# The selected rows of the last four sequences: copied DRAM to DRAM by GpSimd's queue, read by SP as one transfer per unit

## The chip, the core and the metric

The kernel runs on one core of a Trainium2 chip. The core has five engines with an instruction queue each: TensorE (PE, with its weight loads shown apart as PEld), VectorE (DVE), ScalarE (ACT), GpSimd (POOL) and SyncE (SP, which here only issues transfers). Sixteen DMA engines move the data; SP, ACT and POOL hand them transfers on a queue of their own. The metric is the device time of one execution in microseconds, the median of several; less is better.

## The reference

One step of a one-layer decoder for a prompt of 512 tokens and a sample group of 8 sequences with 8 new tokens each, behind 2048 cached tokens. Both groups share the weights. Two attentions run side by side: a forgetting attention ("fox") over all cached keys and a sparse attention ("nsa") with compressed, selected and windowed keys. The cache lies in pages of 128 tokens, named by a page table.

```python
nsa_all = jnp.concatenate([gather_pages(nsa_pool, page_table), pm['nsa_rows']], axis=1)
kc, vc, c_end = compressed_kv(nsa_all[:, :, 0], nsa_all[:, :, 1], lp)
...
ks_blk = to_sel_blocks(nsa_all[:, :, 2], n_sel)
vs_blk = to_sel_blocks(nsa_all[:, :, 3], n_sel)
...
# cache_nsa_kv (DEPTH, N_PHYS, PAGE_SIZE, 4, NSA_GROUPS, HEAD_DIM): [cmp_k raw, cmp_v raw, slc_k, slc_v]
```

A cached row of `cache_nsa_kv` has 512 numbers of 4 bytes: columns 0 to 255 feed the compressed keys, columns 256 to 511 are the selected keys and values, the "selected rows" of the title. The kernel reads all of them for each sequence and masks the blocks that were not selected. A page thus has 128 pieces of 1 KB of selected rows, 128 KB in all; a sequence has 16 pages.

## The kernel before

The program is written with a layer that records all instructions, derives the waits, and puts each engine's instructions in an order by a simulated timeline. Some orders are pinned by hand: `dma` keeps the transfers that one queue issues in the order in which they are written (`issued`), and `link` chains PE's instructions in some stages.

The stages in order of time, by the profile: compressed keys of the cached pages (to about 164 us), projections of x (164 to 293), attention of the prompt (to about 440), attention of the sample (to about 560), merging (to about 715), output projection, MLP.

**Projections.** `run` calls `step(ci)` for ci = 0 to 7. A step multiplies all 576 rows of the normed x by some 260 columns of `w_in`. The product is made from a high and a low part of each operand: `project` splits the weights that were loaded during the step before (`winr`) into `winh` (on ACT) and `winl` (on DVE) in two halves of four slices each, asks for the next step's weights, and then runs 14 times 8 products for PE, tile after tile (`z`). ACT and DVE evict the tiles in turn, the sample's tile into `zS`, which lies in `r1w`. SP's queue carries in each step, in this order: `hfd` (a part of x is put aside, 576 KB), the weights of the next step (1 MB), `adw` (1 MB of `w_ada`), and from `stage()` eight copies of 128 KB: pages of `cache_fox_kv` are copied from DRAM to DRAM into `foxD`, in the layout in which the sample's attention reads them. `stage()` is called eight more times in the prompt's attention. The first instructions of the prompt's attention on POOL are the iotas `kpos` and `cm`, which DVE uses as soon as the projections are over.

**The sample's attention.** Its work is cut into 32 units: unit u is the sequence b = 2 (u // 8) + u % 2 and the quarter i = (u % 8) // 2 of its cached tokens, four pages. `sample_attention` takes two units at a time in 16 rounds s. `key_rows` turns the unit's fox and nsa keys on PE (`k<-identF,rows`), `pair_scores` makes the scores (`ss`), softmax runs on DVE and ACT (`sS`), `values` multiplies with the values, which lie in the same `rows` tile (`so<-rows,spT`). The tiles stand in 11 places that become free as PE finishes with them; `sample_load(u)` asks for unit u in round (u − 9) / 2. A load is one transfer of 512 KB from `foxD` (pieces of 4 KB), and four transfers of 128 KB from the pages of `cache_nsa_kv` (pieces of 1 KB), all on SP's queue. Before the four, SP reads the four page numbers from `ptp` into registers (`by_page`). At three of the 16 units from 16 on (u = 16, 26 and 28) the place is four smaller tiles, and the fox load is two transfers. SP waits before a transfer until the place is free, and until the transfer eight places earlier on its queue has landed.

In the last rounds `hH` (2.3 MB of x, put aside as `hfd`) and the merging's first weights (`graw`, `wbr`, `wmr`) are loaded too.

Of the kernel before, what the change touches and what calls it, by code (L numbers as in the profile page):

```python
# [6 lines left out]
F32 = mybir.dt.float32  # L7
# [7 lines left out]
P = 128  # L15
# [3 lines left out]
NB = 8  # L19
NS = 64  # L20
# [26 lines left out]
class Step:  # L47
# [626 lines left out]
    def stage(self):  # L674

        n = self.staged
        if n == 2 * NB:
            return
        self.staged += 1
        b, q = n // 2, n % 2  # L680
        self.by_page("sync", b, slice(8 * q, 8 * q + 8), lambda p, n: self.dma(
            "sync", self.foxD[b][8 * p:8 * p + 8].rearrange("q (y c) e -> (q y) (c e)", y=2),
            self.I["cache_fox_kv"][0, bass.ds(n, 1)].rearrange("o (q c) e g d -> (o q) (c e g d)", q=16)), 8)

    def stage_logf(self, pe, y):

        row = self.small.tile([P, 1], I32, tag="lfrow", bufs=2, name=f"lfrow{y}")
        self.ts(row, self.ptT, 2.0, float(y), OP.mult, OP.add)
        t = pe.tile([P, 512], F32, tag="lfg", bufs=1, name=f"lfg{y}")
        self.nc.gpsimd.indirect_dma_start(  # L690
            out=t, out_offset=None, in_=self.I["cache_fox_logf"][0].rearrange("n (y t) h -> (n y) (t h)", y=2),
            in_offset=bass.IndirectOffsetOnAxis(ap=row[:, 0:1], axis=0))
        self.lfg[y] = t
# [903 lines left out]
    def sample_load(self, sp, u):  # L1597

        p = u % 11
        where = {27: "6", 28: "5", 29: "8", 30: "9", 31: "a"}.get(u) or "pp23456879a"[p]  # L1600
        if u in (0, 11, 22):
            self.pair = self.keep.tile([P, 2, 2, 4, 256], F32, tag="r2", bufs=1, name=f"rows{u}")
        if where == "p":
            v = [self.pair[:, p]]
        elif where in "45":
            pool, tag = (self.pr, "kst") if where == "4" else (self.pkq, "qst")
            v = [pool.tile([P, 512], F32, tag=tag, bufs=4, name=f"rows{u}{x}").rearrange("p (j n) -> p j n", j=2) for x in range(4)]
        elif where == "3":
            v = [self.pr.tile([P, 2048], F32, tag="cm", bufs=1, name=f"rows{u}").rearrange("p (x j n) -> p x j n", x=2, j=4)]
        elif where == "7":  # L1610
            v = [self.zfp.tile([P, 4 * C_N], F32, tag="zF", bufs=1, name=f"rows{u}")[:, 0:2048].rearrange("p (x j n) -> p x j n", x=2, j=4)]
        else:
            pool = self.pr if where == "2" else self.sp0 if where == "6" else sp
            v = [pool.tile([P, 2, 4, 256], F32, tag="rows" + where, bufs=1, name=f"rows{u}")]
        b, i = 2 * (u // 8) + u % 2, u % 8 // 2
        row = (lambda n, j: v[0][:, n, j]) if len(v) == 1 else (lambda n, j: v[2 * n + j // 2][:, j % 2])
        for x in range(2) if len(v) > 1 else (None,):
            self.dma("sync", v[0][:, 0] if x is None else v[x],
                     self.foxD[b][:, 4 * i:4 * i + 4] if x is None else self.foxD[b][:, 4 * i + 2 * x:4 * i + 2 * x + 2])

        self.by_page("sync", b, slice(4 * i, 4 * i + 4), lambda p, n: self.dma(
            "sync", row(1, p % 4), self.I["cache_nsa_kv"][0, bass.ds(n, 1)].rearrange("o t e g d -> (o t) (e g d)")[:, 256:512]))
        self.rows[u] = row

    def window_load(self, sp, b):
# [878 lines left out]
    def run(self):  # L2504
# [11 lines left out]

        self.hfd = self.tc.dram_tile([P, NK, 2 * NT], F32, name="hfd")
        self.foxD = [self.tc.dram_tile([P, 16, 256], F32, name=f"foxD{b}") for b in range(NB)]
        self.lfD = self.tc.dram_tile([NB, P, P], F32, name="lfD")
        self.staged = 0  # L2520
        self.rows, self.wr, self.soft = {}, {}, {}
# [2 lines left out]
        h2 = []  # L2524
# [40 lines left out]
        with pctx:  # L2565
            pw, pc = self.pw, self.pc
            self.adn, self.ada_open, self.ada_next, self.ada_made = 8, None, None, None

            def step(ci, **kw):
                self.dma("sync", self.hfd[:, ci], h2[ci].bitcast(F32))  # L2570
                self.project(pw, ci, h2, **kw)
                self.ada_later()
                self.stage()

            step(0, between=[lambda: None] + [lambda kv=kv: self.cmp_out(None, 3, kv) for kv in range(2)] + [lambda: self.cmp_keys(3)])
            self.chain = None
            self.cmp_prompt_a(pk, pc)
            self.cmp_prompt_load(pk, 0)
            step(1)
            self.cmp_prompt_b(0)  # L2580
            self.cmp_prompt_load(pk, 1)
            self.head_norm("sk", C_SK, 2, 1)
            self.head_norm("wk", C_WK, 2, 2)
            step(2)
            self.cmp_prompt_b(1)
            self.head_norm("fk", C_FK, 2, 0)
            self.log_sigmoid()
            self.store_rows("fox", (C_FK, 256))
            step(3)
            self.cmp_prompt_c(pc)  # L2590
            self.head_norm("nq0", C_NQ, 4)
            self.gates()
            step(4)
            self.cmp_prompt_d(pc)
            self.head_norm("nq1", C_NQ + 256, 4)
            self.kslc = self.kstack(pk, "slc", C_SK, "w1")
            self.qnsa = {}
            step(5, between=[lambda: None] * 3 + [lambda: self.qnsa.update(self.qstack(self.pkq, "nsa", C_NQ, 1, 0, (0,)))])
            self.cmp_prompt_e(pc)
            self.head_norm("fq0", C_FQ, 4)  # L2600
            step(6, between=[lambda: self.qnsa.update(self.qstack(self.pkq, "nsa", C_NQ, 1, 0, (1,))), lambda: None,
                             lambda: self.sample_q(self.bdN, C_NQ, 1)])
            self.head_norm("fq1", C_FQ + 256, 4)
            step(7, between=[lambda: None] * 3 + [lambda: self.sample_q(self.bdF, C_FQ, 0)])
            self.store_rows("nsa", (C_CK, 256), (C_SK, 128), (C_SV, 128))
            self.store_rows("win", (C_WK, 128), (C_WV, 128))
            self.sample_kv()
# [89 lines left out]
```

## Time and profile before

| | |
|---|---|
| median of 3 runs | 1152.80 us (1152.79 to 1159.15) |
| profiled execution | 1153.68 us, of which 1152.0 us from the first to the last instruction |
| granted clock of TensorE | 0.999 |
| PE busy | 1130.2 us (98%) |
| DVE, ACT, POOL busy | 804.1, 580.5, 278.3 us |
| moved by the DMA engines | 255.5 MB, mean 222 GB/s |

A row of the profile's timeline has the start and the length in us, the engine, the line of the program, the operation, output<-input and shape, and in brackets the time for which the engine was idle before it and what ended that. Lines L78 and L84 are the helpers `mm` and `tr` (PE), L113 is `act`, L132 is `split`, L163 is `dma`: many groups share a line, so they are told apart by their tiles. SPq is SP's queue of instructions.

### The profile page before, as it was taken

What the parts mean: (1) busy time and instruction counts of PE and PEld (TensorE: products, weight loads), DVE (VectorE), ACT (ScalarE), POOL (GpSimd) and SP (SyncE); (2) the same over time, 40 slices, a digit from 0 to 9 for tenths busy, and PEclk for the clock granted to TensorE, in tenths of its full rate; (3) what the DMA queues carried; (4) which work ended last, traced back from release to release, by engine and by line L of the source; (5) the groups of instructions that cost most, each with busy time, mean ns of one, the idle gap of its engine ahead of it and who ended that gap; (6) DMA issues with size and microseconds to landing.
All of it is one profiled execution on the core that took longest, in us unless ns stands there. A gap on an engine that the chain in (4) does not pass through costs nothing.

```text
span 1152.0 us, 25217 instructions
## 1 busy us (share of the span) xinstructions
PE 1130.2 (98%) x9434; PEld 966.1 (84%) x9434; DVE 804.1 (70%) x1937; ACT 580.5 (50%) x1151; POOL 278.3 (24%) x337
## 2 busy tenths in 40 slices
PE   8999999999999999999999999999999999999998
PEld 5888789999756566776899999789999998888887
DVE  4688785687777895776755554677867754798686
ACT  2555463453776785565433223447565655565420
POOL 4302100000220120001576673010656411110100
PEclk9999999999999999999999999999999999999999
DMA  9997456797584779999889996446444637977732
GB/s 223 224 267 227 149 154 201 246 322 233 186 275 143 206 220 315 292 308 327 214 257 304 315 297 222 119 138 216 150 151 149 187 111 254 320 249 263 247 109 83
DMA packets 188188, 255.51 MB, mean 222 GB/s; under 512 B 23161, under 2 KB 144706, under 8 KB 185890
## 3 DMA queue, kind: packets, MB, share of 16 engines
q1 hardware_dynamic: 148770, 173.03, 49.4%
q0 software_dynamic: 21296, 67.38, 18.1%
q10 hardware_dynamic: 18000, 13.50, 3.9%
q8 instruction: 74, 1.21, 0.4%
q14 instruction: 48, 0.39, 0.1%
HBM read 217.64 MB, written 57.12 MB: 238 GB/s over the span
## 4 chain that ended last, share of the span: by engine, by line
PE 83%; DVE 7%; DMA 4%; issue 3%; ACT 2%; SPq 1%; POOL 1%; POOLq 0%; ACTq 0%; DVEq 0%
PE dn L78 14%; PE z L78 9%; PE mg L78 9%; PE hid L78 5%; PE br L78 4%; PE wo L78 4%; PE up L78 3%; PE k L84 2%; PE ct L84 2%; PE ada L78 2%; PE dns L78 2%; DMA rows<-in_cache_nsa_kv 2%; PE ss L78 1%; PE so L78 1%; PE oslc L78 1%
## 5 line engine op out<-in xcount | busy, mean ns | idle before, releaser
L78 PE MATMUL z<-winh,h 128*128 128x264 f32 (+1 forms) x576 | 110.9, 286 | 0.3
L78 PEld LDWEIGHTS z<-winh,h 128*128 128x128 f32 x576 | 91.7, 190 | 2.2 <-DVE h L808 0.9
L78 PE MATMUL z<-winl,h 128*128 128x264 f32 (+1 forms) x320 | 88.1, 284 | 0.0
L113 ACT ACTIVATE xh<-ct 128x256 fp32r<-128x256 f32 x128 | 48.0, 385 | 57.0 <-PE ct L84 32.2
L78 PE MATMUL mg<-hH,wmh 128*128 128x288 f32 x240 | 70.7, 296 | 0.0
L78 PE MATMUL mg<-hH,wml 128*128 128x288 f32 x240 | 70.5, 296 | 0.0
L78 PE MATMUL mg<-hL,wmh 128*128 128x288 f32 x240 | 68.4, 295 | 0.0
L132 DVE TENSOR_TENSOR xl<-ct,xh 128x256 fp32r<-128x256 f32 x128 | 51.8, 421 | 13.2 <-ACT xh L113 11.4
L78 PEld LDWEIGHTS z<-winl,h 128*128 128x128 f32 x320 | 60.6, 190 | 0.0
L132 DVE TENSOR_TENSOR wml<-wmr,wmh 128x1024 fp32r<-128x1024 f32 x14 | 23.4, 1675 | 37.2 <-ACT wmh L113 37.2
L78 PEld LDWEIGHTS mg<-hH,wmh 128*128 128x128 f32 x240 | 45.2, 188 | 0.1
L78 PEld LDWEIGHTS mg<-hH,wml 128*128 128x128 f32 x240 | 45.1, 188 | 0.0
L132 DVE TENSOR_TENSOR wp<-sums,wp 128x1024 fp32r<-128x1024 f32 x26 | 39.0, 1508 | 8.8 <-ACT wp L113 8.2
L78 PEld LDWEIGHTS mg<-hL,wmh 128*128 128x128 f32 x240 | 44.2, 188 | 0.0
L78 PE MATMUL hid<-xh,w1hlv 128*128 128x512 f32 (+1 forms) x160 | 43.6, 359 | 0.4 <-ACT xh L113 0.4
L78 PE MATMUL hid<-xh,w1hlk 128*128 128x512 f32 (+1 forms) x160 | 43.9, 361 | 0.1
L132 DVE TENSOR_TENSOR wp<-pu,wp 128x512 fp32r<-128x512 f32 (+1 forms) x26 | 29.4, 1138 | 17.0 <-ACT wp L113 16.9
L84 PE MATMUL k<-identF,rows 128*128 128x128 f32 x256 | 35.8, 280 | 3.2 <-ACT kt L113 1.5
L2062 POOL TENSOR_TENSOR td<-td,td 128x512 f32<-128x512 f32 x24 | 34.6, 1440 | 13.9 <-DMA td<-in_w_down 13.4
L78 PE MATMUL br<-oL,wbh 128*128 128x288 f32 x128 | 37.7, 295 | 0.0
L78 PE MATMUL br<-oH,wbl 128*128 128x288 f32 x128 | 37.7, 294 | 0.0
L84 PE MATMUL ct<-identF,ro 128*128 128x128 f32 x256 | 35.1, 275 | 2.6 <-DVE ro L116 2.4
(1178 smaller groups left out, 3618.0 us busy)
## 6 DMA issues: line engine op xcount, KB each, us to landing
adw<-in_w_ada SPq DMA_DIRECT2D x16, 1024.0 KB
foxD<-in_cache_fox_kv SPq DMA_DIRECT2D x128, 128.0 KB
rows<-in_cache_nsa_kv SPq DMA_DIRECT2D x128, 128.0 KB
rows<-foxD SPq DMA_DIRECT2D x26, 512.0 KB
pu<-in_w_up SPq DMA_DIRECT2D x26, 512.0 KB
wdr<-in_w_down SPq DMA_DIRECT2D x26, 512.0 KB
cpg<-in_cache_nsa_kv SPq DMA_DIRECT2D x96, 128.0 KB
td<-in_w_down POOLq DMA_DIRECT2D x24, 512.0 KB, 6.6
```

The source lines that it names most:

```text
L78: ins = self.nc.tensor.matmul(out, a, b, start=start, stop=stop, skip_group_check=True)
L84: ins = self.nc.tensor.transpose(out, in_, self.identF[:n, :n])
L113: return self.nc.scalar.activation(out, in_, f, **kw)
L132: self.splits.append((eng or self.nc.vector).tensor_tensor(l, x, h.bitcast(F32), op=OP.subtract).ins)
L2062: self.nc.gpsimd.tensor_tensor(out, x, y, op=OP.subtract)
```

## The change

For sequences 4 to 7 the selected rows are staged, as the fox rows are. At the start of each projection step a new function, `stage_rows(ci, made)`, copies eight pages of one sequence from DRAM to DRAM into `slcD`, on POOL's queue. A small copy (`late`) on POOL, of a number which the step before wrote into `zS`, holds each batch back until that step has left its columns; the first waits for the last part of x. In the sample's attention the units 16 to 31 read their 512 KB of selected rows from `slcD` in one transfer (two of 256 KB at units 16, 26 and 28), in pieces of 4 KB (2 KB). Units 0 to 15 are as before.

```diff
+    def stage_rows(self, ci, made):
+        late = self.small.tile([P, 1], F32, tag="late", bufs=1, name=f"late{ci}")
+        b, q = 4 + ci // 2, ci % 2
+        self.issued["gpsimd"] = self.nc.gpsimd.tensor_copy(late[:NS], made).ins
+        self.by_page("gpsimd", b, slice(8 * q, 8 * q + 8), lambda p, n: self.dma(
+            "gpsimd", self.slcD[b][p // 4, :, p % 4],
+            self.I["cache_nsa_kv"][0, bass.ds(n, 1)].rearrange("o t e g d -> (o t) (e g d)")[:, 256:512]), 8)
...
-        self.by_page("sync", b, slice(4 * i, 4 * i + 4), lambda p, n: self.dma(
-            "sync", row(1, p % 4), self.I["cache_nsa_kv"][0, bass.ds(n, 1)].rearrange("o t e g d -> (o t) (e g d)")[:, 256:512]))
+        if b in self.slcD:
+            for x in range(2) if len(v) > 1 else (None,):
+                self.dma("sync", v[0][:, 1] if x is None else v[2 + x],
+                         self.slcD[b][i] if x is None else self.slcD[b][i, :, 2 * x:2 * x + 2])
+        else:
+            self.by_page("sync", b, slice(4 * i, 4 * i + 4), lambda p, n: self.dma(
+                "sync", row(1, p % 4), self.I["cache_nsa_kv"][0, bass.ds(n, 1)].rearrange("o t e g d -> (o t) (e g d)")[:, 256:512]))
...
+        self.slcD = {b: self.tc.dram_tile([4, P, 4, 256], F32, name=f"slcD{b}") for b in range(4, NB)}
...
             def step(ci, **kw):
                 self.dma("sync", self.hfd[:, ci], h2[ci].bitcast(F32))
+                self.stage_rows(ci, self.zS[:, self.WIN[ci - 1][0]:][:, 0:1] if ci else h2[7][:NS, 0:1].bitcast(F32))
                 self.project(pw, ci, h2, **kw)
```

How instructions move, first on SP, in the sample's attention at unit 17 (the name behind "waits" is what the row waits for; DMAHW are transfers of SP's and ACT's queues, DMASW those of POOL's). Before:

```order
L163 DMA rows_7527<-foxD_84 128x1024 [waits DMAHW3_49,PE_49]
L170 TENSOR_LOAD ptp
L163 ISA
L163 DMA rows_7527<-in_cache_nsa_kv 128x256 [waits DMAHW4_49]
L163 ISA
L163 DMA rows_7527<-in_cache_nsa_kv 128x256 [waits DMAHW5_49]
L163 ISA
L163 DMA rows_7527<-in_cache_nsa_kv 128x256 [waits DMAHW6_49]
L163 ISA
L163 DMA rows_7527<-in_cache_nsa_kv 128x256 [waits DMAHW7_49]
L163 DMA rows_7542<-foxD_83 128x1024 [waits DMAHW0_49,PE_49]
```

And now, from the same unit on:

```order
L163 DMA rows_7736<-foxD_84 128x1024 [waits DMAHW1_49,PE_49]
L163 DMA rows_7736<-slcD_88 128x1024 [waits DMASW3_49,DMASW2_49,DMAHW2_49,DMASW1_49,DMASW0_49]
L163 DMA rows_7739<-foxD_83 128x1024 [waits DMAHW3_49,PE_49]
L163 DMA rows_7739<-slcD_87 128x1024 [waits DMASW7_49,DMASW6_49,DMAHW4_49,DMASW5_49,DMASW4_49]
L163 DMA rows_7875<-foxD_84 128x1024 [waits DMAHW5_49,PE_49]
```

Ten instructions of a unit have become two, and a unit takes two of SP's eight transfers in flight instead of five. A read of `slcD` also waits for the four copies that filled it.

On POOL, at the end of the projections, where the last batch stands. Before, `kpos` and `cm` followed the first iotas:

```order
L126 IOTA Dt 128x132
L126 IOTA kpos 128x512 [waits DMAHW5_49,DMAHW4_49,DMAHW6_49,DMAHW3_49,DMAHW7_49,DMAHW2_49,DMAHW0_49]
L126 IOTA cm 128x128 [waits DMASW6_49,DMASW7_49,DVE_49,PE_49]
L126 IOTA cm 128x128
L1065 TENSOR_SCALAR cm<-cm 128x128 [waits Pool_49]
```

Now the eight batches stand between `Dt` and `kpos`; these are the last two copies and what follows:

```order
L163 ISA
L163 DMA slcD_90<-in_cache_nsa_kv 128x256 [waits DMASW6_49]
L163 ISA
L163 DMA slcD_90<-in_cache_nsa_kv 128x256 [waits DMASW7_49]
L126 IOTA kpos 128x512 [waits DMAHW5_49,DMAHW4_49,DMAHW6_49,DMAHW3_49,DMAHW7_49,DMAHW2_49,DMAHW0_49]
L126 IOTA cm 128x128 [waits PE_49,Activation_49]
L126 IOTA cm 128x128
L1074 TENSOR_SCALAR cm<-cm 128x128 [waits Pool_49]
```

So 8 small copies, 8 reads of page numbers and 64 transfers went in ahead of `kpos` and `cm`, and each copy waits until the one eight places earlier has landed.

On ACT, in step 4 of the projections, where the weights of step 5 (`winr` 0 and 1) are split. Before:

```order
L113 ACTIVATE zN<-z_0_3462 128x256
L113 ACTIVATE r1w<-zN 128x256
L113 ACTIVATE winh_3707<-winr_0_3458 128x1024
L113 ACTIVATE r1w<-zN 128x256
L113 ACTIVATE winh_3707<-winr_1_3460 128x1024
L113 ACTIVATE zN<-z_2_3514 128x256
```

And now:

```order
L113 ACTIVATE zN<-z_0_3601 128x256
L113 ACTIVATE r1w<-zN 128x256 x2
L113 ACTIVATE zN<-z_2_3653 128x256
L113 ACTIVATE r1w<-zN 128x256
L113 ACTIVATE winh_3873<-winr_0_3597 128x1024
L113 ACTIVATE winh_3873<-winr_1_3599 128x1024
L113 ACTIVATE r1w<-zN 128x256
```

Both splits of the weights of step 5 now stand behind the eviction of z tile 2 (`zN<-z_2`) and a square of it. Steps 6 and 7 have similar moves; PE's own order is the same but for a few rows.

## The prediction

> **What bounds the kernel now.** I read the busy table first, then the stretches of the sample's attention, then the gaps of PE in it, then the chain of work behind them.
>
> ```profile
> span 1152.0 us, 25217 instructions
> PE 1130.2 (98%) x9434; PEld 966.1 (84%) x9434; DVE 804.1 (70%) x1937; ACT 580.5 (50%) x1151; POOL 278.3 (24%) x337
> ```
>
> PE is idle for 1152.0 − 1130.2 = 21.8 us in the whole span. No change of transfers can save more than the part of these 21.8 us that waits for transfers. So I ask how many of them lie in the stage whose loads change, and of what they are made.
>
> The view by stretches has length, busy us of PE, PEld, DVE, ACT and POOL, the granted clock, the DMA share and GB/s. The changed loads serve the units 16 to 31, which PE works through from about 500 us to 560 us:
>
> ```profile
> 480.00:520.00 40.00, 39.44 (x874) 29.61 (x864) 26.67 (x89) 23.89 (x54) 1.05 (x2) 1.00 0.93 305
> 520.00:540.00 20.00, 18.87 (x432) 14.02 (x433) 14.67 (x48) 10.73 (x26) 2.15 (x4) 1.00 0.93 309
> 540.00:561.00 21.00, 19.39 (x482) 14.02 (x472) 12.63 (x42) 10.68 (x22) 6.42 (x9) 1.00 0.83 236
> ```
>
> The DMA engines are 83 to 93% busy here, which looks like a memory bound; but PE is idle for only 0.56 + 1.13 + 1.61 = 3.30 us of 81. That is the ceiling of any gain in this stage. PE's timeline has these gaps over 0.25 us (in brackets the idle time and what ended it):
>
> ```profile
> 539.68 0.99 PE L78 MATMUL so<-rows,spT 128*32 128x64 f32 x56 [1.11 <-issue]
> 546.05 0.34 PE L78 MATMUL ss<-DT,E 96*32 96x128 bf16 x6 [0.29 <-issue]
> 551.08 0.33 PE L84 MATMUL k<-identF,rows 128*128 128x128 f32 x1 [0.59 <-DMA rows<-in_cache_nsa_kv]
> 556.54 0.66 PE L84 MATMUL sp<-identF,sS 128*128 128x128 f32 x4 [0.73 <-ACT sS L113]
> ```
>
> Only 0.59 us are a wait for selected rows. 1.11 + 0.29 = 1.40 us are gaps for which the profile names nothing; they fall in the stretch in which hH, the rows and the next weights are fetched together, so a busy DMA may be behind them. 0.73 us is the softmax of the last pair, with nothing left to cover it, and stays.
>
> How the 0.59 us arise, from SP's timeline (start, duration, four page transfers in a row) and the chain of work (start, us):
>
> ```profile
> 527.14 2.85 SPq L163 DMA_DIRECT2D rows<-in_cache_nsa_kv  x4
> 535.10 6.79 SPq L163 DMA_DIRECT2D rows<-in_cache_nsa_kv  x4
> 530.09 10.63 DMA rows<-foxD
> 541.55 9.49 DMA rows<-in_cache_nsa_kv
> ```
>
> SP needs 2.85 us for the four page issues of a unit, and 6.79 us for those of the last one, where it waits for earlier transfers to land. The last page of unit 31 is issued at 541.55 and lands 9.49 us later, just after PE asks for it.
>
> **The change part by part.** *Fewer issues on SP.* 16 units × 4 page transfers become 19 (13 units with one, three with two, since their buffer is in pieces). The issue of one costs little:
>
> ```profile
> L163 SPq DMA_DIRECT2D rows<-in_cache_nsa_kv x128: 332/333/1634, 414.0 to 541.5; - x128
> ```
>
> 45 × 0.33 = 15 us of SP's time go, and with them 16 reads of the page table. SP runs beside PE, so that is no time by itself; its worth is that a unit takes two places among SP's transfers in flight instead of five, and the last units are asked for earlier. The bytes are the same: 16 × 512 KB. Gain: at least 0 (the bytes still pass at the same rate), at most 3.30 − 0.73 = 2.57 us. I take the 0.59 us that the trace ties to these rows and half of the 1.40 us without a name, **−1.3 us**. If the cover goes the other way, and the loads now crowd hH, the cost is bounded by the same few tenths.
>
> *64 copies on POOL's queue during the projections.* Such a DRAM-to-DRAM copy from this queue is not in the trace; the nearest issue is that of the compressed pages at the start, of the same 128 KB, and the first eight of it:
>
> ```profile
> L163 POOL DMA_DIRECT2D cpg<-in_cache_nsa_kv x24: 529/529/809, 20.1 to 40.0; - x24
> 20.10 4.63 POOL L163 DMA_DIRECT2D cpg<-in_cache_nsa_kv  x8 [1.35 <-issue]
> 292.07 0.45 POOL L126 IOTA cm<- 128x128 f32 x2 [125.77 <-PE z L78]
> ```
>
> So a step's batch holds POOL for 0.2 (the copy `late`) + 1.35 (the page numbers) + 4.63 = 6.2 us, eight batches 50 us. POOL is idle for 125.77 us until 292.07, so they are covered there. Behind the last batch stand `kpos` and `cm`, for which DVE and PE wait after the projections. That batch starts when step 6 has left its columns:
>
> ```profile
> 278.00 0.37 ACT L113 ACTIVATE r1w<-z 64x256 f32<-64x256 f32 x1
> 245.78 0.41 DVE L101 TENSOR_TENSOR r1w<-z,r1w 64x256 f32<-64x256 f32 x1
> ```
>
> That is 278.00 + 0.37 + 0.41 = 278.8; 278.8 + 6.2 = 285.0, 7 us before 292.07: **0**.
>
> *The bytes of the copies.* A step copies 8 × 128 KB = 1.05 MB, on DMA engines that are nearly full in steps 4 and 5:
>
> ```profile
> 231.00:246.00 15.00, 15.00 (x138) 14.38 (x138) 11.45 (x37) 7.00 (x17) 0.00 (x0) 1.00 0.94 320
> 246.00:262.00 16.00, 16.00 (x144) 15.05 (x143) 14.50 (x53) 8.23 (x16) 0.00 (x0) 1.00 0.95 314
> 262.00:278.00 16.00, 16.00 (x140) 14.88 (x139) 11.91 (x35) 8.55 (x21) 0.00 (x0) 1.00 0.62 202
> ```
>
> At 314 / 0.95 = 330 GB/s, 1.05 MB take 3.2 us. This rate already holds copies of the same kind (foxD, one MB a step), so 3.2 us is the value that I take. Bounds: 0 where the copies fall into idle time, 6.4 us if read and write each count in full. Who waits for it? The weights of the next step: winr on SP's queue, split by ACT and DVE, then read by PE. Second halves, and the steps' starts on PE (chain of work):
>
> ```profile
> 241.84 1.06 ACT L113 ACTIVATE winh<-winr 128x1024 fp32r<-128x1024 f32 x1 [0.50 <-DMA winr<-in_w_in]
> 242.93 1.23 DVE L132 TENSOR_TENSOR winl<-winr,winh 128x1024 fp32r<-128x1024 f32 x1 [0.31 <-ACT winh L113]
> 254.73 1.23 DVE L132 TENSOR_TENSOR winl<-winr,winh 128x1024 fp32r<-128x1024 f32 x1 [0.15 <-ACT winh L113]
> 266.95 1.23 DVE L132 TENSOR_TENSOR winl<-winr,winh 128x1024 fp32r<-128x1024 f32 x1 [1.65 <-ACT winh L113]
> 246.29 11.51 PE z L78 x96
> 261.71 1.26 PE z L78 x9
> 277.90 11.70 PE z L78 x96
> ```
>
> 96 matmuls in 11.70 us are 0.122 us each. The second half of winh is first read by the 13th, of winl by the 15th: 1.7 us into the step. So the second half of winl is there at 244.16, 255.96 and 268.18, and is wanted at 248.0, 263.4 and 279.6: slack 3.8, 7.4 and 11.4 us for steps 5, 6 and 7. The batch of step 4 meets the weights of step 5, and what it delays stays delayed while the engines are full: delays of 3.2, 6.4 and 9.6 us. All three stay inside the slack, by 0.6, 1.0 and 1.8 us. Earlier batches meet emptier engines. With such thin margins I put **+0.5 us** for the projections, which is about what 4 us a batch would cost (0.2 at step 5, 0.4 at step 6).
>
> *The moved splits.* On ACT the two splits for step 5 now stand behind the eviction of z tile 2:
>
> ```profile
> 242.80 0.36 ACT L113 ACTIVATE zN<-z 128x256 f32<-128x256 f32 x1
> ```
>
> From 242.80: 0.4 for it, 0.4 for the square behind it, 2 × 1.06 and 1.23 give 246.9, still 1.1 us ahead of 248.0: **0**, and no addition to the delay, since ACT then waits for data that is late anyway.
>
> **Sum.** −1.3 + 0.5 = −0.8 us. The profiled execution took 1153.68 us (span 1152.0 and 1.7 around it), 0.88 above the median of 1152.80. So 1152.9 for an execution like it, and **1152.0** for the median.
>
> **Rivals.**
> *The projections become bound by transfers* (the slower side). Place: steps 5 to 7; it decides once a batch costs more than about 3.8 us of DMA time. At the upper bound of 6.4 us: 2.6 us of stall at step 5; at step 6 12.8 − 7.4 − 2.6 = 2.8; at step 7 19.2 − 11.4 − 5.4 = 2.4; together 7.8, so 1152.8 − 1.3 + 7.8 = 1159. For: 94 and 95% DMA share there. Against: foxD's copies already pass there, and PE has no gap.
> *The whole ceiling is won*: all gaps but the softmax tail go and nothing stalls: 1152.8 − 2.57 = 1150.
> *POOL's issues become slow beside DVE.* An issue would have to wait for DVE's copies. POOL has 292.07 − 278.8 − 1.55 = 11.7 us for the last batch, 1.46 us an issue; beyond that each further us an issue delays the start of the prompt's attention by up to 8 us. At 2.5 us: 1152.8 + 8 = 1161.
>
> ```profile
> L116 DVE COPY ro<-cpg x32: 629/689/987, 16.2 to 150.7; 128x1024 f32<-128x1024 f32 x32
> ```
>
> Against it: such copies of DVE ran in the very stretch in which POOL's 24 issues took 0.53 us, at most 0.81. The Trainium skill speaks for this rival: in "SBUF — State Buffer", section "SBUF: two separate sides", a DMA issued from GpSimd can't have its descriptors written while VectorE runs a two-port copy, and its example goes from 620 to 3100 ns; by that, an estimate from the page, eight issues would take 25 us and POOL would be 13 us late. The trace does not agree: 809 ns is the longest.
> *The copies are not used*, or SP waits for them: SP's reads of units 16 to 31 name the copies as their source, and the last copy, issued by 285, is long done at 480. Then the time would be that of before, 1152.8; it gives no other answer than the forecast.
>
> **How the numbers follow.** Forecast (within 2 us of 1152.0) 0.70; whole ceiling 0.10; projections bound 0.16; slow issues 0.02; neither, but the unchanged time 0.02. The range takes in the ceiling below and the upper price of the copies above: 1149.5 to 1159. About 1%, 11.5 us, is the least that a measurement of this kernel can tell from no change. Faster by that much would need over half of PE's 21.8 idle us: 0.01. Slower by over 1% needs prices beyond the upper bound or the slow issues: 0.05. The rest, 0.94, is no change.
>
> **What would show it.** After the change: PE's gap before `k<-identF,rows` near 551 gone; SP's reads of slcD 19 in number, with waits for PE (free buffers) in place of waits for transfers; 64 POOL issues of about 0.53 us ending before 286; DMA share near 1.0 from 231 to 270; ACT's wait for winr longer, but PE without a gap at the starts of steps 5 to 7. A PE wait for winl or winh there of more than 1 us makes the 3.2 us a batch wrong; a POOL row `cm` later than PE's end of z makes the cover wrong.

## The result and the profile after

The changed kernel takes 1166.1 us (median of 7, 1163.1 to 1170.1) against 1155.0 us (median of 7, 1152.8 to 1159.5): ratio 1.0101, 95% interval 1.0081 to 1.0121, slower by 11.7 us (9.4 to 14.0). The prediction had 1152.0 and a range up to 1159.0. The profiled execution took 1167.32 us, with a span of 1165.7. It is compared here with the profile of before, span 1152.0; the busy table first:

```profile
span 1165.7 us, 25259 instructions
PE 1136.9 (98%) x9434; PEld 970.9 (83%) x9434; DVE 797.6 (68%) x1937; ACT 580.2 (50%) x1151; POOL 322.6 (28%) x409
```

PE has the same 9434 matmuls, but is busy for 6.7 us more: a sign that some ran at a lower clock. Its idle time grew by 7.0 us, from 21.8 to 28.8. Where both lie is read from the starts of PE's stages (timeline of PE; first products of the projections, first scores of the prompt's attention, first turned keys of the sample's attention, first matmul of the merging). Before:

```profile
164.26 0.40 PE L78 MATMUL z<-winh,h 128*128 128x264 f32 x2
293.26 0.33 PE L78 MATMUL sslc<-khslc,qstnsa 128*128 128x128 f32 x1
440.52 0.66 PE L84 MATMUL k<-identF,rows 128*128 128x128 f32 x4
560.60 4.55 PE L78 MATMUL mg<-hH,w 128*128 128x288 f32 x32
```

And after:

```profile
164.65 0.40 PE L78 MATMUL z<-winh,h 128*128 128x264 f32 x2
301.26 0.33 PE L78 MATMUL sslc<-khslc,qstnsa 128*128 128x128 f32 x1
449.13 0.66 PE L84 MATMUL k<-identF,rows 128*128 128x128 f32 x4
572.51 4.55 PE L78 MATMUL mg<-hH,w 128*128 128x288 f32 x32
```

The projections take 136.6 us instead of 129.0 (+7.6), the prompt's attention 147.9 instead of 147.3 (+0.6), the sample's attention 123.4 instead of 120.1 (+3.3). The rest of the 13.7 us is 0.4 before the first product and 1.8 in small pieces behind 572 us.

**The projections.** The view by stretches (length, busy PE, PEld, DVE, ACT, POOL, granted clock, DMA share, GB/s), for the stretch in which step 4 begins:

```profile
231.00:246.00 15.00, 10.73 (x64) 10.40 (x64) 8.61 (x30) 6.01 (x15) 4.37 (x9) 0.77 0.98 328
```

PE is idle for 4.3 us of it and runs at a mean clock of 0.77; before, it was busy for all 15.00 at 1.00. Both count: 0.23 of 15 us, some 3.4 us of work, are lost to the clock, and with the idle time that makes the 7.6 us. The waits of PE (us in total, times, longest) name the gap:

```profile
PE z L78 <- ACT winh L113: 4.2, 1, 4.2
```

The chain of work (start, us) shows what it hangs on:

```profile
201.19 10.51 DMA winr<-in_w_in
...
214.44 1.26 DVE winl L132
...
222.81 0.82 DVE zF L101 x4
...
224.68 0.92 SPq L163
225.64 8.50 DMA winr<-in_w_in
234.16 1.06 ACT winh L113
235.27 1.22 PE z L78 x4
236.53 15.53 PE z L78 x108
...
254.29 11.51 PE z L78 x96
```

Read it downwards. The weights of step 3 land at 211.7, and the first split of them follows at 211.78, 4.0 us later than before. Their splits stand on DVE ahead of the normalised fox keys (`zF`), so these are ready at 223.6. SP issues in order: the store of `zF`, `hfd`, and only then the weights of step 4, at 225.64. They take 8.5 us, and PE starts step 4 at 235.27 instead of 230.63. In the kernel before, the rows of ACT (first split of step 3's weights), SP, ACT and DVE at the same place of the timeline read:

```profile
207.78 1.09 ACT L113 ACTIVATE winh<-winr 128x1056 fp32r<-128x1056 f32 x1 [2.48 <-DMA winr<-in_w_in]
...
222.42 1.80 SPq L163 DMA_DIRECT2D winr<-in_w_in  x2
...
228.40 1.06 ACT L113 ACTIVATE winh<-winr 128x1024 fp32r<-128x1024 f32 x1 [3.09 <-DMA winr<-in_w_in]
...
231.27 1.23 DVE L132 TENSOR_TENSOR winl<-winr,winh 128x1024 fp32r<-128x1024 f32 x1
```

So the request is 3.2 us later (0.4 of it because the projections start later), and the transfer takes 8.5 us instead of 6.0: together the first split of step 4's weights is 5.8 us late (234.16 against 228.40). The batches that do this are those of steps 2 and 3; POOL's timeline has the latter right beside the weights of step 4:

```profile
222.60 0.27 POOL L689 COPY late<-r1w 64x1 f32<-64x1 f32 x1 [19.26 <-DVE r1w L101]
223.82 4.52 POOL L163 DMA_DIRECT2D slcD<-in_cache_nsa_kv  x8 [0.95 <-issue]
...
291.97 4.53 POOL L163 DMA_DIRECT2D slcD<-in_cache_nsa_kv  x8 [0.18 <-issue]
...
300.13 0.45 POOL L126 IOTA cm<- 128x128 f32 x2 [3.05 <-PE z L78]
```

The last two rows answer for the cover: the last batch is issued by 296.5, and `cm` still waits for PE. From step 5 on PE has no gap; each step starts 8.0 us later than before (254.29 against 246.29).

**The sample's attention.** First by stretches:

```profile
480.00:520.00 40.00, 36.59 (x806) 26.75 (x805) 26.91 (x91) 21.12 (x49) 2.14 (x4) 0.98 0.88 315
520.00:540.00 20.00, 20.00 (x419) 14.84 (x418) 12.18 (x39) 10.70 (x22) 0.00 (x0) 0.96 0.80 281
```

And PE's gaps over 0.3 us with no name, from its timeline:

```profile
490.41 0.22 PE L78 MATMUL ss<-DT,E 96*32 96x128 bf16 x1 [1.46 <-issue]
...
508.87 0.66 PE L84 MATMUL k<-identF,rows 128*128 128x128 f32 x4 [0.42 <-issue]
...
516.62 0.53 PE L78 MATMUL so<-rows,spT 128*32 128x64 f32 x19 [1.53 <-issue]
...
546.99 0.41 PE L78 MATMUL so<-rows,spT 128*32 128x64 f32 x11 [0.34 <-issue]
```

The wait for selected rows near 551 us is gone. But the gaps for which the profile names nothing are now 1.46 + 0.42 + 1.53 + 0.34 = 3.75 us instead of 1.40, and the clock is at 0.98 and 0.96 instead of 1.00, which over 40 and 20 us is 1.6 us of work. In this profile 2.35 us more of such gaps and 1.6 us of clock, less the 0.59 us of the wait that went, are the 3.3 us. In the second profile of the kernel before (in the table below) the wait of 0.59 us is absent too, and the gap of 1.11 us is one of 0.20, so that they went is not by itself an effect of the change.

The 0.6 us of the prompt's attention stand in all ten profiles with batches of full size in steps 6 and 7 (147.8 to 147.9 us), and in none of the other six (147.2 to 147.4); their cause was not followed up.

### The profile page after: what moved, and what is told of

It reads as the page before. It is cut to its first block, busy times and chain, and to the rows that moved or that the text cites. A ratio compares the mean times of both kernels' runs of the same rounds, so it can differ in the third digit from the quotient of the medians.

```text
span 1165.7 us, 25259 instructions
## 1 busy us (share of the span) xinstructions
PE 1136.9 (98%) x9434; PEld 970.9 (83%) x9434; DVE 797.6 (68%) x1937; ACT 580.2 (50%) x1151; POOL 322.6 (28%) x409
## 4 chain that ended last, share of the span: by engine, by line
PE 82%; DVE 8%; DMA 5%; ACT 2%; issue 2%; SPq 0%; ACTq 0%; DVEq 0%
PE dn L78 12%; PE mg L78 9%; PE z L78 7%; PE hid L78 7%; PE br L78 4%; PE wo L78 4%; PE up L78 3%; PE k L84 3%; PE ct L84 2%; PE ss L78 2%; PE so L78 2%; DMA winr<-in_w_in 2%; PE ada L78 1%; PE sp L84 1%; PE oslc L78 1%
## 5 line engine op out<-in xcount | busy, mean ns | idle before, releaser
L78 PE MATMUL z<-winh,h 128*128 128x264 f32 (+1 forms) x576 | 113.6, 291 | 4.5 <-ACT winh L113 4.2
L132 DVE TENSOR_TENSOR wml<-wmr,wmh 128x1024 fp32r<-128x1024 f32 x14 | 19.0, 1356 | 41.4 <-ACT wmh L113 41.4
L2076 POOL TENSOR_TENSOR td<-td 128x512 f32<-128x512 f32 x24 | 36.9, 1542 | 15.9 <-DMA td<-in_w_down 15.7
L113 ACT ACTIVATE mgt<-mg 128x288 f32<-128x288 f32 x32 | 12.5, 407 | 52.9 <-PE mg L78 52.9
L113 ACT ACTIVATE u<-u 128x1152 f32<-128x1152 f32 x29 | 33.7, 1160 | 9.3 <-DVE u L101 8.7
```

Source lines behind the costliest of these rows:

```text
L78: ins = self.nc.tensor.matmul(out, a, b, start=start, stop=stop, skip_group_check=True)
L113: return self.nc.scalar.activation(out, in_, f, **kw)
L132: self.splits.append((eng or self.nc.vector).tensor_tensor(l, x, h.bitcast(F32), op=OP.subtract).ins)
L2076: self.nc.gpsimd.tensor_tensor(out, x, y, op=OP.subtract)
```

## Experiments

Theory A: there are two separate losses. The bytes of the copies make the weights of step 4 late, which costs the 7 to 8 us of the projections; the reads in the sample's attention cost something of their own. Rivals: the whole loss comes from the copies; it comes from the reads; not the bytes but the added issues and the shifted order do it. The table has the length of two stages (from the profile of each, as above) and the timed ratio to the kernel before.

| kernel | projections, us | sample's attention, us | ratio (95% interval) |
|---|---|---|---|
| before, two profiles | 129.0, 129.3 | 120.1, 118.9 | 1 |
| changed, two profiles | 136.6, 136.0 | 123.4, 122.1 | 1.0101 (1.0081 to 1.0121) and 1.0091 (1.0057 to 1.0124) |
| copies alone | 135.4 | 119.2 | 1.0071 (1.0044 to 1.0099) |
| reads alone | 129.8 | 118.1 | 1.0014 (0.9993 to 1.0035) |
| copies alone, a quarter of the bytes | 129.5 | 121.5 | 1.0028 (1.0006 to 1.0050) |
| copies alone, without steps 2 and 3 | 130.3 | 121.1 | 1.0028 (1.0003 to 1.0053) |
| copies alone, step 2 only | 132.5 | 119.5 | 1.0037 (1.0007 to 1.0066) |
| copies alone, step 3 only | 132.1 | 118.0 | 1.0022 (0.9999 to 1.0046) |
| whole change, batches behind the weights | 129.8 | 121.6 | 1.0043 (1.0028 to 1.0058) |
| whole change, batches moved | 129.1, 129.1 | 120.3, 121.3 | 1.0013 (0.9990 to 1.0037) and 1.0009 (0.9985 to 1.0034) |
| the same, pieces of 1 KB | 129.0 | 120.2 | 1.0019 (0.9997 to 1.0041) |
| batches moved, page reads | 129.3 | 120.6 | 1.0010 (0.9988 to 1.0031) |
| whole change, gap filled | 137.1 | 121.0 | 1.0090 (1.0054 to 1.0126) |

**Copies alone and reads alone.** The copies alone keep the page reads:

```diff
-        if b in self.slcD:
+        if False:
```

> The copies alone; the sample's attention reads the pages as before, and nothing reads the staged rows. Theory A (two separate losses: the copies make the weights of step 4 late, and the new reads of the sample's attention cost on their own): the projections end 8 us later, the sample's attention takes as long as before, so about +8 us on the kernel before (ratio near 1.007), with PE's 4 us gap before step 4 and a granted clock of 0.5 behind it. Theory B (everything comes from the copies, the loss in the sample's attention is only its echo): +12 us, ratio 1.010. Theory C (everything comes from the reads): no change.

The reads alone leave `stage_rows` out and read `foxD` twice:

```diff
-                self.stage_rows(ci, self.zS[:, ...)
...
-                         self.slcD[b][i] if x is None else self.slcD[b][i, :, 2 * x:2 * x + 2])
+                         self.foxD[b][:, 4 * i:4 * i + 4] if x is None else self.foxD[b][:, 4 * i + 2 * x:4 * i + 2 * x + 2])
```

> The reads alone: no copies, and units 16 to 31 read the same 512 KB of foxD a second time in place of their selected rows (so their selected keys and values are others). Theory A: the projections as before; the sample's attention 2 to 4 us longer, with PE gaps of over 1 us that the profile puts down to issue; ratio 1.002 to 1.003. My prediction's own step (fewer transfers on SP gain up to 1.3 us): ratio 0.999. Theory C: +12 us.

The copies alone cost 8.2 us by their ratio, with the same gap ahead of step 4 (PE's timeline), and leave the sample's attention as it was:

```profile
236.40 0.78 PE L78 MATMUL z<-winh,h 128*128 128x256 f32 x4 [3.96 <-ACT winh L113]
```

The reads alone cost nothing that can be told from no change (0.8 us less to 4 us more). In their profile the sample's attention took 118.1 us, 2.0 less than in the first profile of before and 0.8 less than in its second; the merging took 4.5 us more, with PE waiting for `oL` from DVE, which also happened in two other kernels (below). So the projections' part of theory A holds; a cost of the reads in this order of size does not show here.

**Bytes or issues.** A quarter of the rows of each page, with all 64 issues:

```diff
-            "gpsimd", self.slcD[b][p // 4, :, p % 4],
+            "gpsimd", self.slcD[b][p // 4, 0:32, p % 4],
...
-            ...rearrange("o t e g d -> (o t) (e g d)")[:, 256:512]), 8)
+            ...rearrange("o t e g d -> (o t) (e g d)")[0:32, 256:512]), 8)
```

> The copies alone, as in the run of the copies alone, with the same 64 issues on GpSimd's queue and the same waits, but only 32 of the 128 rows of a page are copied, so a quarter of the bytes (nothing reads them). Theory A (bytes): a batch takes 0.8 us of DMA time in place of 3.2, the weights of step 4 are at most 1.6 us late, PE's gap ahead of step 4 stays under 2 us and the clock stays at 1: ratio 1.000 to 1.002. Rival (the number of transfers on a second queue, or the order that the added instructions give the other engines): as the copies alone, ratio 1.007.

PE is busy through the whole stretch in which it waited, at full clock:

```profile
231.00:246.00 15.00, 15.00 (x132) 14.12 (x131) 10.43 (x32) 7.29 (x18) 4.16 (x9) 1.00 0.96 321
```

The projections take 129.5 us: it is the bytes (or the pieces of 1 KB, whose number fell with them), not the issues. The ratio is above what I expected. In its profile the merging took 162.6 us instead of 154, with PE waiting for `oL` from DVE; but that execution, of 1167.6 us, was the slowest of the ten, and where the median of 1159.9 us lost its 3 us (0.7 to 5.8) is not shown. The merging took 154.1 to 154.9 us in all other profiles but two (157.4, 158.6), also between two executions of the same kernel (154.2 and 157.4 with the batches moved), so the merging varies between single executions; the cause was not looked for.

**Which batches.** First without those of steps 2 and 3, then each of the two by itself (all with page reads):

```diff
-                self.stage_rows(ci, self.zS[:, ...)
+                if ci not in (2, 3):    # then: if ci == 2, if ci == 3
+                    self.stage_rows(ci, self.zS[:, ...)
```

> As the copies alone, but without the batches of steps 2 and 3 (sequence 5 isn't staged; the pages are read as before). Theory A, with the delay made by the batches of steps 2 and 3: step 4 starts as before, and the batches of steps 4 to 7 stay within the slack that I worked out for steps 5 to 7: no change, ratio within 0.001 of 1. Rival (each batch costs its share): 6 of 8 batches leave 6 of the 8 us, ratio 1.005.

> The copies alone, and of them only the batch of step 2 (nothing reads it). Theory A in its parts: this batch makes the weights of step 3 some 3 to 4 us late; their splits stand on DVE ahead of the norm of the fox keys, so out_fox and behind it the request for the weights of step 4 go out 3 us late on SP. Without the batch of step 3 nothing more is added: PE has a gap of 1 to 2.5 us ahead of step 4, under the length that lowers the clock; projections 130.5 to 132 us (before 129.0, with all copies 135.4 to 136.6), ratio 1.001 to 1.003. Rival (only the batch of step 3 counts, since it runs beside the weights of step 4): 129 us.

> The copies alone, and of them only the batch of step 3 (nothing reads it). Theory A: without the batch of step 2 everything of step 2 is in time, so this batch is released at about 219 us, in a stretch in which the DMA engines are nearly idle (share 0.01 to 0.29 at 214 to 222 us before), and is through before or soon after the weights of step 4 are asked for at 222.4: gap ahead of step 4 at most 1 us, projections 129 to 130 us, ratio 1.000 to 1.001. Rival (only the batch of step 3 counts): a gap of 3 us or more, projections 133 us or more.

Without the two, the projections lose 1.3 us instead of 6.4, and step 4 has no gap: six of the eight batches are nearly free there. The ratio of 1.0028 is above the expected 1.001, with an interval that reaches down to 1.0003; what it holds besides the 1.3 us is not shown. By itself, the batch of step 2 (SP's rows, then ACT's and PE's):

```profile
225.68 1.80 SPq L163 DMA_DIRECT2D winr<-in_w_in  x2
...
231.07 1.06 ACT L113 ACTIVATE winh<-winr 128x1024 fp32r<-128x1024 f32 x1 [4.03 <-DMA winr<-in_w_in]
...
232.18 0.78 PE L78 MATMUL z<-winh,h 128*128 128x256 f32 x4 [1.00 <-ACT winh L113]
233.44 0.39 PE L78 MATMUL z<-winl,h 128*128 128x256 f32 x1 [0.48 <-DVE winl L132]
```

And the batch of step 3:

```profile
222.97 1.11 SPq L163 DMA_DIRECT2D winr<-in_w_in  x2
...
232.10 1.06 ACT L113 ACTIVATE winh<-winr 128x1024 fp32r<-128x1024 f32 x1 [6.24 <-DMA winr<-in_w_in]
...
233.21 0.78 PE L78 MATMUL z<-winh,h 128*128 128x256 f32 x4 [2.03 <-ACT winh L113]
234.47 0.38 PE L78 MATMUL z<-winl,h 128*128 128x256 f32 x1 [0.48 <-DVE winl L132]
```

With step 2's batch the request goes out 3.3 us late (225.68) but the transfer is as quick as before (5.4 us); with step 3's the request is nearly in time (222.97) but the transfer takes 9.1 us. In both profiles the projections start 0.5 to 0.6 us later than in the first profile of before. The first batch delays through DVE and SP, the second through the DMA engines. The price of a batch is read from the transfers: step 3's batch makes the transfer of step 4's weights 3.1 us longer, and its own packets fill 29.5% of the 16 engines' time from 223 to 234 us, that is 3.2 us; step 2's batch makes the first split of step 3's weights 4.0 us later (211.8 against 207.8), or 3.4 without the later start.

What the projections lose, 3.5 and 3.1 us, comes near the same figure partly by chance. Step 2's 3.5 us are 1.5 of idle time and 2.0 in step 4's products, at a lower clock; step 3's 3.1 are 2.5 of idle time and 0.6 in the products. So the expectation for step 2's batch had the chain and the gap right, but not the clock, and its 130.5 to 132 us became 132.5. The expectation for step 3's batch failed: I had it released at 219 and through before or soon after the request; it was released at 219.9 and issued from 221.1 to 225.7, on both sides of the request at 222.97.

**Other places.** The whole change, first with `late` reading the next step's `winr`, then with four batches at the end of the compressed keys (issued from 137 to 163 us), two in steps 0 and 1 and two in steps 6 and 7:

```diff
-                self.stage_rows(ci, self.zS[:, ...)
                 self.project(pw, ci, h2, **kw)
+                self.stage_rows(ci, self.wraw[ci + 1][1][:NS, 0, 0:1] if ci < 7 else self.zS[:, ...)
```

> The whole change, but the small copy of step ci reads the second half of winr of step ci + 1, so a batch starts only when those weights have landed. Theory A: step 4 starts on PE within 0.5 us of before, the 8 us in the projections go, and the loss of the sample's attention stays: +2 to +4 us on the kernel before, ratio 1.002 to 1.004. Rival (the 8.4 MB as such cost the projections, wherever a batch falls: 8 x 3.2 us of DMA time on nearly full engines): adw and foxD push the next weights back instead, and step 5 or 6 has the gap; ratio 1.006 or more.

```diff
+        for k, u in enumerate((34, 35, 36, 38)):
+            todo[u] += [lambda k=k: self.stage_rows(k, self.ring[0][1][:NS, 0, 0:1].bitcast(F32))]
...
-                self.stage_rows(ci, self.zS[:, ...)
+                if ci in (0, 1, 6, 7):
+                    self.stage_rows(ci if ci > 5 else 4 + ci, self.zS[:, ...)
```

> The whole change, with the same eight batches at other places: four at the end of the compressed keys (from about 135 us, DMA share 0.5 and below in the trace of before), two in steps 0 and 1, two in steps 6 and 7; none in steps 2 to 5. Theory A: the projections take 129 us as before (136.6 in the changed kernel, 129.8 with the batches held behind the weights); what is left is the sample's attention, between the 2.0 us that the reads alone gained and the 3.3 us that the changed kernel lost there: ratio 0.998 to 1.002. Rival (a batch costs wherever it stands): ratio 1.004 or more, as with the batches held behind the weights.

Both free the projections (129.8 and 129.1 us). In the first all 8.4 MB still pass there, so the bytes as such cost at most 0.8 us. The moved batches are 0.8 to 0.9% faster than the changed kernel and not to be told from the kernel before; no version ran faster than that one. The first variant is still 5 us slower (3.2 to 6.7), of which 0.8 lie in the projections and 1.5 in the sample's attention of its profile; the rest is not pinned down.

**What is left: the reads.** A second profile of the changed kernel, the staged rows in pieces of 1 KB (`slcD` page by page, still one transfer a unit), and, with the moved batches, page reads against staged reads:

> The changed kernel once more, for a second profile: does the loss of the sample's attention (123.4 us against 120.1) come back with PE gaps of over 1 us that end on issue, each just behind a transfer of PE's instructions, or do these gaps fall elsewhere in each execution? If they belong to the reads in pieces of 4 KB: again 2 to 4 us of such gaps between 480 and 560 us. If they are chance: another sum, and the stage within 1 us of 120. Projections: again 136 to 137 us, ratio 1.010.

```diff
-        self.slcD = {b: self.tc.dram_tile([4, P, 4, 256], ...
+        self.slcD = {b: self.tc.dram_tile([4, 4, P, 256], ...
...
-            "gpsimd", self.slcD[b][p // 4, :, p % 4],
+            "gpsimd", self.slcD[b][p // 4, p % 4],
...
-                         self.slcD[b][i] if x is None else ...)
+                         (self.slcD[b][i] if x is None else ...).rearrange("j p e -> p j e"))
```

> As the moved batches, but the staged rows lie page by page, so that the reads of units 16 to 31 are still one transfer of 512 KB, in pieces of 1 KB as before the change. If the PE gaps on issue come from bursts of 4 KB pieces that fill the DMA engines (over 400 GB/s, share 1.0) while PE's instructions are fetched: no such gap over 0.5 us between 440 and 545 us, and the stage takes 119 to 120 us. If the number of transfers matters (fewer, larger ones): as the moved batches. Ratio 0.998 to 1.001.

> The moved batches (four at the end of the compressed keys, two in steps 0 and 1, two in steps 6 and 7), but the sample's attention reads the pages as before, and nothing reads the staged rows. This is the other half of the comparison with the moved batches: only the reads of units 16 to 31 differ. If the staged reads cost something of their own: this kernel is 1 to 3 us faster than the moved batches with staged reads, and its sample's attention takes 118 to 121 us. If the staged reads gain what I predicted: it is 1.3 us slower. Ratio on the kernel before 0.999 to 1.001.

> The moved batches with the staged reads once more, beside the same kernel with page reads. If the staged reads cost: the sample's attention again above 120 us (120.2 to 123.4 so far), ratio 1.001 to 1.003. If they gain 1.3 us: below the kernel with page reads, ratio under 1.

Timed, page and staged reads can't be told apart: 1.0010 and 1.0009, each uncertain by about 0.0023, which is more than the 1.3 us that I had predicted. By the profiles in the table, the stage took 120.2 to 123.4 us with reads of `slcD` (seven profiles, mean 121.4) and 118.0 to 121.5 us with page reads (eight, mean 119.9); the reads alone, which read `foxD` in the same pieces, took 118.1. A wait of PE for selected rows stands in three of the eight (0.6 to 2.3 us) and in none of the seven, so the staged reads do seem to remove it. A cost of 1 to 2 us in the stage may be there all the same; a gain does not show, and the timing alone could not exclude one of 1.3 us. The gaps on issue of the second profile of the changed kernel, then of the pieces of 1 KB:

```profile
508.86 0.66 PE L84 MATMUL k<-identF,rows 128*128 128x128 f32 x4 [2.07 <-issue]
...
515.52 0.53 PE L78 MATMUL so<-rows,spT 128*32 128x64 f32 x19 [0.43 <-issue]
...
545.29 0.41 PE L78 MATMUL so<-rows,spT 128*32 128x64 f32 x11 [0.89 <-issue]
```

```profile
538.20 0.41 PE L78 MATMUL so<-rows,spT 128*32 128x64 f32 x10 [1.32 <-issue]
```

They come at the same places of PE's program as in the first profile (`k` x4, `so` x19, `so` x11), inside runs of equal instructions, with other lengths each time. Pieces of 1 KB do not remove them (1.32 us), so that expectation failed too. In the traces of all 16 profiles, each of the 42 such gaps of 0.2 us or more in this stage ends 1.2 to 1.8 us behind the end of one of the 16 KB transfers of instructions, which pass through the same DMA engines, some 6 us apart. So these gaps are most likely waits of PE for its instructions, with the page reads too; but no run here changes those transfers, so this is not shown by experiment, and why the staged reads should lengthen the waits stays open.

**The clock behind the gap.** 20 matmuls into a bank that nothing reads, between the last work ahead of step 4 and its first product:

```diff
+        if ci == 4:
+            with self.tc.issue_after(self.last_z):
+                self.cmp_warm(20)
```

> The whole change, and 20 more matmuls of 128x512 bf16 into a bank that nothing reads, between the last PE work ahead of step 4 and its first product (4.3 us by the same matmuls at the start). They fill the gap in which PE waits for the weights. If the granted clock of 0.5 behind the gap is a result of the idle time: the clock stays at 1, the products of step 4 take 13.4 us again, and the projections take 133 us in place of 136.0 to 136.6: ratio 3 us lower, 1.007. If the clock is something else (the DMA load, chance), the projections stay at 136 us or more.

PE's rows:

```profile
230.21 4.48 PE L78 MATMUL idle<-identB 128*128 128x512 bf16 x20
235.19 0.51 PE L78 MATMUL z<-winh,h 128*128 128x256 f32 x2 [0.49 <-ACT zN L113]
...
253.32 0.50 PE L78 MATMUL z<-winh,h 128*128 128x256 f32 x2 [0.43 <-DVE zN L116]
```

And the stretch:

```profile
231.00:246.00 15.00, 13.94 (x99) 11.31 (x97) 8.97 (x30) 5.60 (x14) 4.39 (x9) 1.00 0.97 328
```

Without the idle time the clock stays at 1.00, so the drop follows from it. But the time did not come back: the projections took 137.1 us and not the expected 133. Ahead of the gap this profile is 0.7 us earlier than that of the changed kernel; at the end of step 4's products it is 2.1 us ahead, and at the start of step 5 again only 0.7, after new waits for evictions (0.43 us above, 0.50 just before), for which the bank that the filling takes may be to blame. What the low clock costs in the end is thus not settled; within the gap's step it is 3.4 us (from 235.27 to 252.06, 16.8 us for the products of step 4, against 13.4 before).

## Why the prediction was wrong

- **Fewer issues on SP, −1.3 us: not borne out.** SP's reads of `slcD` are 19, and the 0.59 us wait for rows near 551 went, as forecast; but it is not in the second profile of the kernel before either. The 1.40 us without a name, of which I took half as won, did not go: such gaps are 3.75 us in the profile, and by the instruction transfers behind which they end they were hardly waits for rows. The moved batches, which leave only the reads to count, are 0.1% slower than before, uncertain by 0.2%.
- **The batches on POOL, 0: right.** The issues took 0.52 to 0.60 us. They ended at 296.5 us and not before 286, since the steps came 8 us later; `cm` still waited for PE. This also settles the rival of slow issues beside DVE: nothing like 1.46 us occurred.

```profile
L163 POOL DMA_DIRECT2D slcD<-in_cache_nsa_kv x64: 523/523/596, 169.6 to 296.0; - x64
```

- **The bytes, +0.5 us: the price was right, the place was wrong.** 3.2 us a batch stands against 3.1 us (step 3's batch) and 3.4 us (step 2's) by which one batch by itself delayed a transfer of weights. For steps 5 to 7 the slack held: without the batches of steps 2 and 3, the four of steps 4 to 7 gave PE no wait for weights. The step that failed is the sentence "Earlier batches meet emptier engines", which put the earlier batches at nothing; the projections lost 7.6 us in place of 0.5. I worked out the slack of steps 5, 6 and 7 and not that of step 4. The row was there: the second half of `winl` ends at 231.27 + 1.23 = 232.5, and is wanted 1.7 us behind the step's start at 230.63, that is at 232.3. By that rule step 4 has no slack at all, and the engines are not emptier where it counts. In the kernel before, by stretches:

```profile
202.00:214.00 12.00, 12.00 (x113) 11.25 (x114) 8.88 (x36) 4.79 (x10) 0.00 (x0) 1.00 1.02 336
214.00:222.00 8.00, 8.00 (x81) 7.83 (x78) 5.80 (x33) 4.28 (x9) 0.00 (x0) 1.00 0.13 30
222.00:234.00 12.00, 12.00 (x108) 11.25 (x108) 6.03 (x19) 5.81 (x16) 0.00 (x0) 1.00 1.01 333
```

  A DMA share of 0.81 over 200 to 240 us looked like room, but it is full, empty, full, and both full stretches are those in which weights come. Two batches of 3.2 us come close to the 5.8 us by which the first split of step 4's weights was late.
- **The order of the queues was not followed.** I followed each batch to the next step's weights, and took a delay there to be a delay of PE only. The batch of step 2 found no waiting PE at step 3, but moved DVE's splits, DVE's work behind them, and through SP's in-order queue the request for the weights of step 4. It also moved its own successor: batch 3 is released by step 2's last columns (`late` at 222.60 instead of 219.9 with that batch alone).
- **The moved splits on ACT, 0: right.** No gap at the starts of steps 5 to 7.
- **The rivals.** "The projections become bound by transfers" named the right mechanism, and that its 7.8 us are near the 7.6 measured is luck: it stood at steps 5 to 7, with a deciding price of 3.8 us a batch, where none of it occurred. At step 4 any price decides. With 0.16 for it, and a range that ended at its 1159 with the reads' gain taken off, the outcome of 1166 had no place.
- **What would show it.** The line that a wait of over 1 us for `winh` makes the batch's price wrong misled in one point: the wait came, a step earlier, with the price right.
- **A lower clock behind a gap** was no term of the sum. Of the 7.6 us of the projections 4.2 are the gap ahead of step 4, and 3.4 are step 4's products at the lower clock.

## What to carry to other kernels

When a transfer is added to a stage with double-buffered weights, work out the slack of every step, from the rows of its last split and of its first use, and above all of the steps in which the DMA engines look idle: a mean share says nothing about the moment at which the next weights are asked for. Follow a late transfer through the in-order queues of the engines that consume it, since what stands behind it may be the request for the next one. Copies that only have to be done some time belong in a stretch that is empty and asks for nothing; here this alone took back all of the projections' 7 us, and a gain at the reading end still did not show.

## What the hardware showed beside this

PE's clock halved after idle time that was shorter than I had expected, and not after other idle time that was longer. The changed kernel behind its gap of 4.2 us (from 242 us on the clock was at 1.00 again):

```profile
236.00:238.00 2.00, 1.96 (x10) 1.67 (x9) 2.00 (x5) 1.92 (x5) 0.00 (x0) 0.50 1.13 386
```

With step 2's batch alone, behind gaps of 1.00 and 0.48 us (rows above), and then with step 3's alone, behind 2.03 and 0.48:

```profile
234.00:236.00 2.00, 2.00 (x13) 2.00 (x12) 2.00 (x6) 1.35 (x5) 0.00 (x0) 0.59 1.11 420
```

```profile
234.00:236.00 2.00, 1.53 (x12) 1.53 (x13) 2.00 (x5) 1.89 (x4) 0.00 (x0) 1.00 1.14 401
```

The shorter gap lowered the clock and the longer one did not. In the sample's attention a gap of 1.53 us lowered it (0.96 over 520 to 540 us, above), and one of 2.07 us, in the second profile of the changed kernel, left it at 1.00. The Trainium skill, in "TensorE: Matmul & The Clock Gate", Part 1, says that the clock goes to one half after an idle window of about 3.4 us, and that the window runs freely. The half agrees with the 0.50 here; the length does not: here 1.00 + 0.48 us of idle time, or 1.53 us, were enough.
